# Experts: one more weight chunk in two parts, and the turns of rows at other chunks

## The chip, the cores and the metric

The kernel runs on one core of one Trainium2 chip. Its time is device microseconds of one execution; a figure for a kernel is the median of several executions. All rows below come from one further execution, taken with the hardware profiler.

## The reference

One layer of a streaming encoder: 512 rows of width 1024 in float32. Attention in two head groups comes first, then a mixture of 16 experts. The change is in the experts. What has to be computed there, cut to its core:

```
h2 = _rms(x, norm2_g) * (1.0 + sc2) + sh2
gate = ...                      # top-1 of 4 groups, top-2 of its 4 experts, softmax weights
for e in range(16):
    he = silu(h2 @ w_gate[e]) * (h2 @ w_up[e])      # 1024 -> 512, twice
    y = y + gate[:, e:e+1] * (he @ w_down[e])       # 512 -> 1024
x = x + g2 * y
```

Each expert has 6 MB of weights, some 100 MB in all; they pass through the core once.

## The kernel before

The rows that chose an expert are gathered into one tile of up to 128 rows (`gather_rows`, an indirect DMA of POOL), turned by TensorE so that the features lie on the partitions (`turn`), and written as a high and a low part. The result is scaled by the gate and added to the output by an indirect DMA (`scatter`).

The weights of one expert are 12 **chunks** of 128x1024 values: `g0` to `g3`, `u0` to `u3` (gate and up, two blocks of 128 features each) and `d0` to `d3` (down). The list `CH` sets their order; in the steady part it repeats `u0..u3` of expert e, `g0..g3` of expert e+1, `d0..d3` of expert e. These 12 chunks are called a cycle here. A prime marks the gate chunks of the next expert: g0' to g3'.

A chunk is multiplied in one of two ways:

- **Split.** `chunk_split` (lines 1579 and 1580) makes a high part on ScalarE (`A.copy`, a CAST to fp32r) and a low part on VectorE (`V.tensor_tensor`, a subtraction). `mm3` (lines 235 to 237) then multiplies high by high, low by high and high by low: six matmuls of 512 columns for a chunk.
- **Whole.** The chunk stays in float32 as loaded, and line 1901 multiplies it with the rows in float32: two matmuls, which the trace shows as four records. ScalarE and VectorE do nothing for it. `whole` names the chunks treated so.

Splitting runs four chunks ahead of the matmuls (`AHEAD`). The parts lie in a ring of 11 tiles (`hw`), of which two belong to one chunk; one is given away to a result tile. `late_split` is a table by chunk c: it says whether the split of chunk c+4 is issued before the matmuls of c or after them, and with that where the split stands in the queues of ScalarE and VectorE. Nothing else sorts this part: every engine takes its instructions in the order in which the code issues them.

`raw_load` brings two chunks (1 MB) from memory into one of 12 places; `raw_next` issues the load that reuses a place as soon as both its chunks are used up, so for a split chunk after its split and for a whole chunk after its matmuls.

Five other pieces stand between the chunks:

- `turn(e, q)` for q = 0 and 1: four transposes on TensorE (line 1710), four ACTIVATEs and a CAST on ScalarE (1695, 1697), a subtraction on VectorE (1698, tile `xl`). The half q = 1 feeds chunks 2 and 3 of gate and up.
- `turn_act(e)` after `g1'`: four transposes of the activation (line 1870), a CAST on ScalarE (1873) and a subtraction on VectorE (1874), tile `he`.
- `silu` on ScalarE after `g3` (1924), and the product with the up result on VectorE after `u3` (1927, tile `sl`).
- the `slot_chain` of a later expert: a comparison on VectorE (1658, tile `oh`), four small matmuls (1662, tile `ps_po`), five small instructions on VectorE (1633 to 1640).
- after `d3` two scalings on VectorE (1962, tile `y`) and the scatter.

Of the kernel before, what the change touches and what calls it, by code (L numbers as in the profile page):

```python
# [89 lines left out]
def tile_trunk(ctx, tc, t, out):  # L90
# [45 lines left out]
    def drop(*tiles):  # L136
        for r in tiles:
            ring, k = owner.pop(r.tensor.name)
            spare[ring].append(k)
# [1381 lines left out]

    def whole(nm, j):

        return nm + str(j) in ('g3', 'u3')

    rawt, wsp, held, used = {}, {}, {}, {}
    slots, xs_, eb = {}, {}, {}
# [33 lines left out]
    def raw_next(c):  # L1561

        e, nm, j = CH[c]
        r = RAWS.index((e, nm, j // 2)) + len(PLACES)
        used[r] = used.get(r, 0) + 1
        if used[r] == 2 and r < len(RAWS):
            raw_load(r)

    def chunk_split(c):
        e, nm, j = CH[c]  # L1570
        parts = rawt[e, nm, j // 2][j % 2]
        if whole(nm, j):
            wsp[c] = parts
            return
        hi, lo = wsp[c] = [take("hw", [1024], F32R, n) for n in ("whi", "wlo")]
        n = 1024 // len(parts)
        for k, src in enumerate(parts):
            s = slice(k * n, k * n + n)
            A.copy(hi[:, s], src)  # L1579
            V.tensor_tensor(lo[:, s], src, f32(hi[:, s]), op=OP.subtract)  # L1580
        raw_next(c)
# [16 lines left out]
    def gather_rows(e):  # L1598
        gather(xs_["g"][:, e % 2, :], slots[e][0])
# [12 lines left out]
    def short_values():  # L1612

        v = eb["v16"] = rt.rearrange("p a b c d -> p (a b c d)")[:, 0:NT * NE * 5 // 2].bitcast(BF16).rearrange(
            "p (j e c) -> p j e c", j=NT, e=NE)
        ij = take("t1", [2, NT, NE], name="ij")
        G.iota(ij[:, 0], pattern=[[0, NT], [0, NE]], base=0, channel_multiplier=1, allow_small_or_imprecise_dtypes=True)
        G.iota(ij[:, 1], pattern=[[1, NT], [0, NE]], base=1, channel_multiplier=0, allow_small_or_imprecise_dtypes=True)
        r, f = (take("t1", [NT, NE], name=nm) for nm in ("rest", "part"))
        V.tensor_copy(v[:, :, :, 0:2].rearrange("p j e c -> p c j e"), ij)  # L1620
        src = tv[:, :, :, 2]
        for c in (2, 3, 4):
            V.tensor_copy(v[:, :, :, c], src)
            if c < 4:
                V.tensor_copy(f, v[:, :, :, c])
                V.tensor_tensor(r, src, f, op=OP.subtract)
                src = r
        drop(ij, r, f)
# [20 lines left out]
    def slot_chain(e):  # L1649
        yield need("D", "t2", ("rank", 0))  # L1650
        short = e >= 2
        oh = take("t2", [NT, CAP], BF16 if short else F32, name="oh")

        def sel(lo, hi):

            n = hi - lo
            i3 = iota1.rearrange("p (o w) -> p o w", o=1).broadcast_to([P, n, CAP])
            V.tensor_tensor(oh[:, lo:hi, :], i3, rkp[:, lo:hi, e:e + 1].broadcast_to([P, n, CAP]), op=OP.is_equal)

        def add(j):  # L1660
            v = eb["v16"][:, j, e, :] if short else tv[:, j, e, :]
            PE.matmul(pst[:, 0:v.shape[-1]], oh[:, j, :], v, start=(j == 0), stop=(j == NT - 1))

        if e < 2:
            sel(0, 2)
        if e == 0:
            eb["oh"] = oh
            mark("oh0")
        yield need("D", "", ("rank", 2))
        sel(2 if e < 2 else 0, NT)  # L1670
        if e == 0:
            mark("oh")
        yield need("P", "po", ("gates", 0), ("gates", 2))
        pst = take("po")
        for j in range(NT):
            add(j)
        if e:
            drop(oh)
        yield need("D")
        slots[e] = slot_rows_short(pst, small, e + 1 == NE) if short else slot_rows(pst, small)  # L1680
        drop(pst)
        mark("slots", e)
# [162 lines left out]
    def now(chain):  # L1845
        for _ in chain:
            pass
# [28 lines left out]

    last = []

    late_split = {'u3': 1, 'g2': 1, 'g1': 1, 'd3': 1, 'd1': 1, 'g0': 1}
    pend = []  # L1880
    ahead, ys = {}, []
    yy = page(6, [2, D], name="y")
    for c, (e, nm, j) in enumerate(CH):
        if c + AHEAD < len(CH) and not late_split.get(nm + str(j), 0):
            chunk_split(c + AHEAD)
        late = late_split.get(nm + str(j), 0)
        if c == 0:
            short_values()
        for e1 in range(2, NE):
            d = c - max(12 * e1 - 38, e1 - 2)  # L1890
            if d == 0:
                ahead[e1] = slot_chain(e1)
            for _ in range({0: 3, 3: 1, 4: 1}.get(d, 0)):
                next(ahead[e1], None)
            if e1 == 2 and d == 4:
                gather_rows(2)
        hi, lo = (wsp.pop(c) * 2)[:2]
        if whole(nm, j):
            for kk in range(2):
                src = hi[:, kk * 512:kk * 512 + 512] if hi is lo else (hi, lo)[kk]  # L1900
                PE.matmul(eb[nm, e], eb["xf", e][:, 2 * j + kk - 4, :], src, start=(j == 0 and kk == 0), stop=(j == 3 and kk == 1))  # L1901
            raw_next(c)
            if (nm, j) == ("u", 3):
                drop(eb["xf", e])
        elif nm != "d":
            if j == 0:
                eb[nm, e] = take("mm")
            for kk in range(2):
                kt = 2 * j + kk
                cs = slice(kk * 512, kk * 512 + 512)  # L1910
                mm3(eb[nm, e], xs_["h"][:, e % 2, kt, :], xs_["l"][:, e % 2, kt, :], hi[:, cs], lo[:, cs], kt == 0, kt == 7)
        else:
            if j == 0:
                eb["y", e] = [take("sc"), take("sc")]
            for n in range(2) if e + 1 < NE else (0,):
                cs = slice(n * 512, n * 512 + 512)
                mm3(eb["y", e][n], xs_["he"][:, 0, j, :], xs_["he"][:, 1, j, :], hi[:, cs], lo[:, cs], j == 0, j == 3)
            if e + 1 == NE:
                last.append((hi, lo))
        if not whole(nm, j) and (nm, e) != ("d", NE - 1):  # L1920
            drop(hi, lo)
        if (nm, j) == ("g", 3):
            eb["sl", e] = take("t2", [FE], name="sl")
            A.activation(eb["sl", e], eb["g", e], AF.Silu)
            drop(eb["g", e])
        if (nm, j) == ("u", 3):
            V.tensor_tensor(eb["sl", e], eb["sl", e], eb["u", e], op=OP.mult)
            drop(eb["u", e])
            if e + 1 == NE:
                turn_act(e)  # L1930
        for q in range(2):
            for e1 in (1,) if e < 1 else (e, e + 1, e + 2):
                if e1 >= NE or e1 < 1:
                    continue
                at = ((0, "u", 1 + q)) if e1 == 1 else ((e1 - 1, 'g', 3), (e1 - 1, 'u', 0))[q]
                if at == (e, nm, j):
                    now(turn(e1, q))
                    if q == 1 and e1 + 2 < NE:
                        gather_rows(e1 + 2)
        if (nm, j) == ('g', 1) and e >= 1 and e - 1 + 1 < NE:  # L1940
            turn_act(e - 1)
        if c + AHEAD < len(CH) and late:
            if late == 2:
                pend.append(c + AHEAD)
            else:
                chunk_split(c + AHEAD)
        if late < 2:
            while pend:
                chunk_split(pend.pop(0))
        if (nm, j) == ("d", 0) and e == 3:  # L1950
            count_rounds()
        elif (nm, j) == ("d", 3):
            if e < 3:
                ys.append(take("hw", [D], name="y") if e == 2 else yy[:, e, :])
            y = ys[e % 3]
            for n in range(2):
                cs = slice(n * 512, n * 512 + 512)
                if e + 1 == NE and n:
                    scatter(slots[e][2], y, 0)
                    for k, (hi, lo) in enumerate(last):  # L1960
                        mm3(eb["y", e][n], xs_["he"][:, 0, k, :], xs_["he"][:, 1, k, :], hi[:, cs], lo[:, cs], k == 0, k == 3)
                V.scalar_tensor_tensor(y[:, cs], eb["y", e][n], slots[e][1], rows["g2"][:, cs], op0=OP.mult,  # L1962
                                       op1=OP.mult)
            drop(*eb["y", e])
            if e + 1 == NE:
                scatter(slots[e][3], y, 1)
            else:
                scatter(slots[e][0], y)
# [105 lines left out]
```

## Time and profile before

| what | value |
|---|---|
| time, median of 3 runs | 678.45 us (676.32 to 679.75) |
| time of the profiled execution | 679.67 us |
| its span, first to last instruction | 678.0 us |
| TensorE busy (matmuls) | 639.6 us, 94% |
| VectorE busy | 554.9 us, 82% |
| ScalarE busy | 433.3 us, 64% |
| GpSimd busy | 157.9 us, 23% |
| mean granted TensorE clock | 0.975 of full speed |

The profiled execution lasts 1.67 us longer than its span and stands 1.22 us above the median of the three runs. Shares are means over the whole span; the experts take the last 317 us of it, and there the shares are others. A matmul's record overlaps the next one's, since the engine is pipelined: the distance from start to start is what a matmul costs, not its recorded length. The same holds, by less, for VectorE.

### The profile page before, as it was taken

The page shows a single profiled execution, that of the slowest core. Times are in us where ns is not written, and L with a number is a line of the kernel's source. Part 1 is how long each engine was busy: PE and PEld are TensorE (multiplying, and loading weights), DVE is VectorE, ACT ScalarE, POOL GpSimd, SP SyncE. Part 2 cuts the span into 40 slices and gives each one's busy share as a digit, 9 for nine tenths or more (in the row PEclk, how much of TensorE's full clock was granted, in tenths as well). Part 3 has the DMA queues.
Part 4 walks back from the last instruction along what each step waited for, and adds up shares of the span by engine and source line. Part 5 has one row for each costly group of instructions (what it writes and reads, how often), then busy time and mean ns, then how long its engine had stood idle before and what let it go on. Part 6 is the DMA issues. An engine that isn't in the chain of part 4 may idle for free.

```text
span 678.0 us, 10463 instructions
## 1 busy us (share of the span) xinstructions
PE 639.6 (94%) x3465; PEld 505.5 (75%) x3465; DVE 554.9 (82%) x1229; ACT 433.3 (64%) x835; POOL 157.9 (23%) x230
## 2 busy tenths in 40 slices
PE   8998899999989999999999999999999999999991
PEld 7666798998777876767787677777777777777761
DVE  5768887898887677789988888998988888888870
ACT  6575555755664454433477877777787778777750
POOL 2653021266120001132010111222211022231121
PEclk9798789999998999999999999999999999999996
DMA  8789454036322545237789999999999999999522
GB/s 310 250 249 299 146 194 126 6 102 208 110 71 63 186 175 208 93 125 253 312 309 382 375 346 371 367 370 388 382 395 375 384 368 375 373 370 374 155 31 33
DMA packets 61931, 169.67 MB, mean 250 GB/s; under 512 B 8807, under 2 KB 23629, under 8 KB 54576
## 3 DMA queue, kind: packets, MB, share of 16 engines
q1 hardware_dynamic: 56448, 154.02, 61.2%
q0 software_dynamic: 5376, 14.93, 9.7%
q8 instruction: 28, 0.46, 0.3%
q14 instruction: 31, 0.25, 0.1%
q10 hardware_dynamic: 48, 0.01, 0.0%
HBM read 159.63 MB, written 15.49 MB: 258 GB/s over the span
## 4 chain that ended last, share of the span: by engine, by line
PE 53%; DVE 10%; DMA 3%; ACT 2%; issue 2%; POOL 0%; POOLq 0%; DVEq 0%; ACTq 0%
PE ps_mm L1901 8%; PE ps_mm L235 7%; PE ps_mm L237 7%; PE ps_mm L236 7%; PE ps_sc L235 4%; PE ps_sc L237 4%; PE ps_sc L236 4%; PE ps_tp L1710 2%; DVE acc L1238 2%; DMA xg<-h_d,idx 1%; PE ps_po L887 1%; PE ps_sc L860 1%; PE ps_tp L1870 1%; PE ps_sc L1088 1%; PE ps_tp L874 1%
## 5 line engine op out<-in xcount | busy, mean ns | idle before, releaser
L1580 DVE TENSOR_TENSOR wlo<-wraw,whi 128x1024 fp32r<-128x1024 f32 (+1 forms) x168 | 190.3, 1170 | 8.9 <-ACT whi L1579 8.8
L1579 ACT CAST whi<-wraw 128x1024 fp32r<-128x1024 f32 (+1 forms) x168 | 157.9, 1005 | 0.9 <-PE ps_sc L237 0.5
L1609 POOL DMA_INDIRECT out_dram<-y,idx x15 | 39.9, 2659 | 216.3 <-DVE y L1962 216.3
L235 PE MATMUL ps_mm<-whi,xh 128*128 128x512 f32 x192 | 84.3, 439 | 0.0
L237 PE MATMUL ps_mm<-whi,xl 128*128 128x512 f32 x192 | 75.4, 393 | 0.0
L236 PE MATMUL ps_mm<-wlo,xh 128*128 128x512 f32 x192 | 75.0, 391 | 0.0
L1901 PE MATMUL ps_mm<-wraw,xf 128*128 128x512 f32 x128 | 60.2, 592 | 0.0
L1695 ACT ACTIVATE xf<-ps_tp,norm2x 128x128 f32<-128x128 f32 x120 | 45.1, 462 | 18.2 <-PE ps_tp L1710 18.2
L235 PE MATMUL ps_mm<-whi,hT_hi 128*128 128x256 f32 x192 | 56.7, 295 | 0.0
L236 PE MATMUL ps_mm<-wlo,hT_hi 128*128 128x256 f32 x192 | 55.0, 287 | 0.6 <-DVE wlo L223 0.6
L237 PE MATMUL ps_mm<-whi,hT_lo 128*128 128x256 f32 x192 | 54.8, 285 | 0.0
L235 PE MATMUL ps_sc<-whi,he 128*128 128x512 f32 x128 | 52.8, 412 | 0.7 <-ACT he L1873 0.7
L1238 DVE SCALAR_TENSOR_TENSOR acc<-adaw,s_c,acc 128x512 f32<-128x512 f32 x60 | 47.0, 791 | 4.6 <-DMA adaw<-in_w_ada_dram 3.8
L237 PE MATMUL ps_sc<-whi,he 128*128 128x512 f32 x128 | 50.2, 392 | 0.0
L236 PE MATMUL ps_sc<-wlo,he 128*128 128x512 f32 x128 | 49.9, 390 | 0.0
L236 PEld LDWEIGHTS ps_mm<-wlo,xh 128*128 128x128 f32 x192 | 36.2, 189 | 9.8 <-issue 3.3
L235 PEld LDWEIGHTS ps_mm<-whi,xh 128*128 128x128 f32 x192 | 36.1, 188 | 9.7 <-issue 3.6
L237 PEld LDWEIGHTS ps_mm<-whi,xl 128*128 128x128 f32 x192 | 36.0, 188 | 8.3
L236 PEld LDWEIGHTS ps_mm<-wlo,hT_hi 128*128 128x128 f32 x192 | 37.3, 194 | 1.0 <-DVE wlo L223 0.9
L235 PEld LDWEIGHTS ps_mm<-whi,hT_hi 128*128 128x128 f32 x192 | 37.3, 194 | 0.3
L1873 ACT CAST he<-ps_tp 128x512 fp32r<-128x512 f32 x16 | 9.4, 587 | 43.7 <-PE ps_tp L1870 43.7
L237 PEld LDWEIGHTS ps_mm<-whi,hT_lo 128*128 128x128 f32 x192 | 37.2, 194 | 0.0
(443 smaller groups left out, 1475.0 us busy)
## 6 DMA issues: line engine op xcount, KB each, us to landing
wraw<-in_w_gate_dram SPq DMA_DIRECT2D x32, 1024.0 KB
wraw<-in_w_down_dram SPq DMA_DIRECT2D x32, 1024.0 KB
wraw<-in_w_up_dram SPq DMA_DIRECT2D x24, 1024.0 KB
adaw<-in_w_ada_dram SPq DMA_DIRECT2D x32, 512.0 KB
wraw<-in_w_ada_dram SPq DMA_DIRECT2D x8, 1024.0 KB
wraw<-in_w_up_dram SPq DMA_DIRECT2D x32, 256.0 KB
wraw<-in_w_in_dram SPq DMA_DIRECT2D x12, 512.0 KB
wo<-in_w_o_dram SPq DMA_DIRECT2D x8, 512.0 KB
```

The costliest lines, as they stand in the source:

```text
L235: PE.matmul(o, xh, wh, start=first, stop=False)
L236: PE.matmul(o, xh, wl, start=False, stop=False)
L237: PE.matmul(o, xl, wh, start=False, stop=last)
L860: PE.matmul(s_[:, z * W:(z + 1) * W], qT[h // 4][0:QK + NT, h % 4, qs], kT[h // 4][0:QK + NT, h % 4, 0:W], start=True, stop=True)
L1238: V.scalar_tensor_tensor(acc[0], w[:, z, :], sc, acc[0], op0=OP.mult, op1=OP.add)
L1579: A.copy(hi[:, s], src)
L1580: V.tensor_tensor(lo[:, s], src, f32(hi[:, s]), op=OP.subtract)
L1609: G.indirect_dma_start(out=o, out_offset=bass.IndirectOffsetOnAxis(ap=idx[:, :1], axis=0), in_=y[:, cs], in_offset=None, compute_op=OP.add)
L1695: A.activation(xf[:, kk, :], p3[:, kk, :], AF.Identity, scale=gc, bias=sc)
L1710: PE.transpose(pt[:, kk * P:(kk + 1) * P], xs_["g"][:, e % 2, k0:k0 + P], ident)
L1873: A.copy(xs_["he"][:, 0], p3)
L1901: PE.matmul(eb[nm, e], eb["xf", e][:, 2 * j + kk - 4, :], src, start=(j == 0 and kk == 0), stop=(j == 3 and kk == 1))
```

## The change

Three things change, all in the experts. `g3` leaves the set of whole chunks and is split like the others; `u3` alone stays whole. The table `late_split` has other entries, and the stages of `slot_chain` come one chunk later. The two turns of an expert's rows move: the first from after `g3'` to after `d2` of the same cycle, two experts ahead; the second from after `u0` to after `u2` of the expert before.

```diff
--- before.py
+++ after.py
@@ -1521,7 +1521,7 @@
 
     def whole(nm, j):
 
-        return nm + str(j) in ('g3', 'u3')
+        return nm + str(j) in ('u3',)
 
     rawt, wsp, held, used = {}, {}, {}, {}
     slots, xs_, eb = {}, {}, {}
@@ -1876,7 +1876,7 @@
 
     last = []
 
-    late_split = {'u3': 1, 'g2': 1, 'g1': 1, 'd3': 1, 'd1': 1, 'g0': 1}
+    late_split = {'u3': 1, 'd1': 1, 'g1': 1, 'u0': 1}
     pend = []
     ahead, ys = {}, []
     yy = page(6, [2, D], name="y")
@@ -1887,12 +1887,12 @@
         if c == 0:
             short_values()
         for e1 in range(2, NE):
-            d = c - max(12 * e1 - 38, e1 - 2)
+            d = c - max(12 * e1 - 37, e1 - 2)
             if d == 0:
                 ahead[e1] = slot_chain(e1)
-            for _ in range({0: 3, 3: 1, 4: 1}.get(d, 0)):
+            for _ in range({0: 3, 4: 1, 5: 1}.get(d, 0)):
                 next(ahead[e1], None)
-            if e1 == 2 and d == 4:
+            if e1 == 2 and d == 5:
                 gather_rows(2)
         hi, lo = (wsp.pop(c) * 2)[:2]
         if whole(nm, j):
@@ -1929,10 +1929,10 @@
             if e + 1 == NE:
                 turn_act(e)
         for q in range(2):
-            for e1 in (1,) if e < 1 else (e, e + 1, e + 2):
+            for e1 in (e, e + 1, e + 2):
                 if e1 >= NE or e1 < 1:
                     continue
-                at = ((0, "u", 1 + q)) if e1 == 1 else ((e1 - 1, 'g', 3), (e1 - 1, 'u', 0))[q]
+                at = ((0, "u", 1 + q)) if e1 == 1 else ((e1 - 2, 'd', 2), (e1 - 1, 'u', 2))[q]
                 if at == (e, nm, j):
                     now(turn(e1, q))
                     if q == 1 and e1 + 2 < NE:
```

The first place is TensorE in the ninth cycle, around `g3'`. `whi` and `wlo` are the parts of a split chunk, `wraw` an unsplit one, `xf` the rows in float32, `xh` and `xl` their parts. Before:

```order
L1870 MATMUL ps_tp_7120<-ident,sl_6978 128x128 x4
L235 MATMUL ps_mm_7103<-whi_7088,xh_5429 128x512
L236 MATMUL ps_mm_7103<-wlo_7089,xh_5429 128x512
L237 MATMUL ps_mm_7103<-whi_7088,xl_5430 128x512
L235 MATMUL ps_mm_7103<-whi_7088,xh_5429 128x512
L236 MATMUL ps_mm_7103<-wlo_7089,xh_5429 128x512
L237 MATMUL ps_mm_7103<-whi_7088,xl_5430 128x512
L1901 MATMUL ps_mm_7103<-wraw_6795,xf_7066 128x512 x2
L1710 MATMUL ps_tp_7157<-ident,xg_5312 128x128 x4
L235 MATMUL ps_sc_7173<-whi_7110,he_5431 128x512
L236 MATMUL ps_sc_7173<-wlo_7111,he_5431 128x512
L237 MATMUL ps_sc_7173<-whi_7110,he_5431 128x512
```

The same place in the changed kernel, from the second half of `g2'` on:

```order
L235 MATMUL ps_mm_7185<-whi_7145,xh_5435 128x512
L236 MATMUL ps_mm_7185<-wlo_7146,xh_5435 128x512
L237 MATMUL ps_mm_7185<-whi_7145,xl_5436 128x512
L235 MATMUL ps_mm_7185<-whi_7175,xh_5435 128x512
L236 MATMUL ps_mm_7185<-wlo_7176,xh_5435 128x512
L237 MATMUL ps_mm_7185<-whi_7175,xl_5436 128x512
L235 MATMUL ps_mm_7185<-whi_7175,xh_5435 128x512
L236 MATMUL ps_mm_7185<-wlo_7176,xh_5435 128x512
L237 MATMUL ps_mm_7185<-whi_7175,xl_5436 128x512
L235 MATMUL ps_sc_7241<-whi_7181,he_5437 128x512
L236 MATMUL ps_sc_7241<-wlo_7182,he_5437 128x512
L237 MATMUL ps_sc_7241<-whi_7181,he_5437 128x512
```

Between `g2'` and `d0` there stood the two float32 matmuls of line 1901 and the transposes of a turn; now there stand six matmuls of a split chunk, and the turn has gone.

The second place is VectorE in the same cycle, from the product after `u3` on. Before:

```order
L1927 TENSOR_TENSOR sl_6978<-sl_6978,ps_mm_7054 128x512
L1580 TENSOR_TENSOR wlo_7111<-wraw_6773,whi_7110 128x1024
L1874 TENSOR_TENSOR he_5431<-ps_tp_7120,he_5431 128x512
L1580 TENSOR_TENSOR wlo_7128<-wraw_6773,whi_7127 128x1024
L1658 TENSOR_TENSOR oh_7133<-iota_307,rkp 128x512
L1580 TENSOR_TENSOR wlo_7142<-wraw_6791,whi_7141 128x1024
L1580 TENSOR_TENSOR wlo_7146<-wraw_6791,whi_7145 128x1024
L1698 TENSOR_TENSOR xl_5430<-xf_7162,xh_5429 128x512
L1580 TENSOR_TENSOR wlo_7170<-wraw_6838,whi_7169 128x1024
```

The same stretch now, with one row before it:

```order
L1698 TENSOR_TENSOR xl_5436<-xf_7160,xh_5435 128x512
L1927 TENSOR_TENSOR sl_7050<-sl_7050,ps_mm_7122 128x512
L1580 TENSOR_TENSOR wlo_7176<-wraw_6805,whi_7175 128x1024
L1580 TENSOR_TENSOR wlo_7182<-wraw_6835,whi_7181 128x1024
L1874 TENSOR_TENSOR he_5437<-ps_tp_7198,he_5437 128x512
L1580 TENSOR_TENSOR wlo_7206<-wraw_6835,whi_7205 128x1024
L1580 TENSOR_TENSOR wlo_7212<-wraw_6851,whi_7211 128x1024
L1580 TENSOR_TENSOR wlo_7222<-wraw_6851,whi_7221 128x1024
L1658 TENSOR_TENSOR oh_7227<-iota_307,rkp 128x512
L1580 TENSOR_TENSOR wlo_7238<-wraw_6885,whi_7237 128x1024
L1580 TENSOR_TENSOR wlo_7256<-wraw_6885,whi_7255 128x1024
L1580 TENSOR_TENSOR wlo_7262<-wraw_5493,whi_7261 128x512
```

Behind the product (`sl`) there was one subtraction for the weights ahead of `he`, now there are two; the turn's `xl`, which stood between the subtractions for `d` and those for `u`, stands right before the product, and the comparison `oh` comes behind all four subtractions for `d`.

## Rows read from the trace of the kernel before

**Rows 1.** The page: the span of the profiled execution.

```profile
span 678.0 us, 10463 instructions
```

**Rows 2.** Windows: PE, PEld, DVE, ACT, POOL busy us (instructions), clock, DMA share, GB/s.

```profile
480.00:500.00 20.00, 20.00 (x92) 15.01 (x91) 17.73 (x24) 15.98 (x25) 4.41 (x2) 1.00 1.02 386
620.00:640.00 20.00, 20.00 (x88) 15.11 (x87) 17.09 (x19) 15.02 (x23) 2.29 (x1) 1.00 0.75 242
640.00:660.00 20.00, 18.54 (x77) 13.22 (x76) 15.90 (x17) 11.65 (x14) 4.55 (x1) 1.00 0.23 38
```

**Rows 3.** Waits, 380 to 640 us: us in total, times, longest.

```profile
ACT he L1873 <- PE ps_tp L1870: 35.1, 13, 2.7
...
DVE he L1874 <- ACT he L1873: 13.3, 14, 1.1
DVE wlo L1580 <- ACT whi L1579: 7.7, 30, 0.3
...
DVE xl L1698 <- ACT xh L1697: 5.9, 14, 0.9
```

**Rows 4.** Timeline of PE: start, us, line, operation, count.

```profile
482.39 0.39 PE L235 MATMUL ps_mm<-whi,xh 128*128 128x512 f32 x1
...
483.76 0.60 PE L1710 MATMUL ps_tp<-ident,xg 128*128 128x128 f32 x4
...
486.97 1.88 PE L1901 MATMUL ps_mm<-wraw,xf 128*128 128x512 f32 x4
488.28 0.79 PE L235 MATMUL ps_mm<-whi,xh 128*128 128x512 f32 x1
...
491.82 0.48 PE L235 MATMUL ps_mm<-whi,xh 128*128 128x512 f32 x1
...
493.29 1.88 PE L1901 MATMUL ps_mm<-wraw,xf 128*128 128x512 f32 x4
495.00 0.60 PE L1710 MATMUL ps_tp<-ident,xg 128*128 128x128 f32 x4
...
496.83 0.25 PE L1662 MATMUL ps_po<-rt,oh 128*128 128x5 bf16 x4
496.95 0.48 PE L235 MATMUL ps_sc<-whi,he 128*128 128x512 f32 x1
...
501.12 0.39 PE L235 MATMUL ps_mm<-whi,xh 128*128 128x512 f32 x1
```

**Rows 5.** Timeline of DVE in the same expert.

```profile
483.74 0.16 DVE L1633 COPY sv<-ps_po 128x5 f32<-128x5 f32 x1
...
484.40 1.41 DVE L1962 SCALAR_TENSOR_TENSOR y<-ps_sc,gate,g 128x512 f32<-128x512 f32 x2
485.73 1.22 DVE L1580 TENSOR_TENSOR wlo<-wraw,whi 128x1024 fp32r<-128x1024 f32 x1
486.86 0.68 DVE L1698 TENSOR_TENSOR xl<-xf,xh 128x512 fp32r<-128x512 f32 x1
487.53 2.36 DVE L1580 TENSOR_TENSOR wlo<-wraw,whi 128x1024 fp32r<-128x1024 f32 x2
489.81 0.68 DVE L1927 TENSOR_TENSOR sl<-sl,ps_mm 128x512 f32<-128x512 f32 x1
490.41 1.22 DVE L1580 TENSOR_TENSOR wlo<-wraw,whi 128x1024 fp32r<-128x1024 f32 x1
```

**Rows 6.** Timeline of ACT in the same expert.

```profile
484.39 1.50 ACT L1695 ACTIVATE xf<-ps_tp,norm2x 128x128 f32<-128x128 f32 x4 [1.25 <-PE ps_tp L1710]
485.93 0.62 ACT L1697 CAST xh<-xf 128x512 fp32r<-128x512 f32 x1
```

**Rows 7.** Timeline of PE, first expert: the turn of the second expert's rows.

```profile
371.47 0.63 PE L1710 MATMUL ps_tp<-ident,xg 128*128 128x128 f32 x4 [0.15 <-DMA xg<-h_d,idx]
```

**Rows 8.** Timeline of POOL: the gather that this turn waits for.

```profile
362.12 1.11 POOL L1602 DMA_INDIRECT xg<-h_d,idx  x1 [17.17 <-DVE idx L1595]
```

**Rows 9.** Timeline of ACT near the end: a cast of loaded weights.

```profile
651.48 1.06 ACT L1579 CAST whi<-wraw 128x1024 fp32r<-128x1024 f32 x1 [0.30 <-PE ps_mm L237]
```

## The prediction

> **What bounds the kernel now.** Read first the windows of the expert stage, then the waits of the same stretch, then the timelines of one cycle on each engine.
>
> In a window of 20 us in the middle of the experts TensorE is busy for all 20.00 us at the full granted clock, VectorE for 17.73, ScalarE for 15.98 [rows 2]. Among the waits from 380 to 640 us those of ScalarE and VectorE are for each other or for TensorE, while none of TensorE's own comes near theirs (those that matter here: [rows 3]). So the matmuls set the pace, and VectorE comes next.
>
> The timeline of TensorE gives the cycle: `u0` starts at 482.39 and again at 501.12, so an expert costs 18.73 us [rows 4]. What a piece costs is the distance between starts. The whole chunk `g3'` starts at 493.29 and the turn behind it at 495.00: 1.71 us. Split chunks: `u0` from 482.39 to 483.76 is 1.37; `d1` to `d3` from 496.95 to 501.12 are 4.17, so 1.39 each; `g2'` from 491.82 to 493.29, right behind transposes, is 1.47. The turn before `u1` starts at 483.76.
>
> **The change part by part.**
>
> *TensorE.* In each cycle four float32 records (1.71 us) become six split matmuls. I take 1.39 for them, the mean of three chunks in a row; the ends are 1.37 and 1.47. That saves 0.32 a chunk (0.24 to 0.34). The turns, `he`'s transposes and the small matmuls of line 1662 remain in number and only stand elsewhere. The first turn now stands right before line 1662, where a pause behind it may fall together with the one there: `g2'` behind transposes costs 0.08 more than the mean chunk, so up to 0.1 a cycle is possible; I take none.
>
> How many count: 16 `g3` are split, but the first one's gain is lost. In the first cycle the turn of the second expert's rows starts at 371.47, and the row says that it waited for the gather [rows 7], which POOL issued at 362.12 once VectorE had the row numbers [rows 8]. Those instructions are the same as before, and the chunks ahead of the turn will only wait longer. That leaves 15 x 0.32 = 4.8 us (15 x 0.24 = 3.6 to 15 x 0.44 = 6.6). The new cycle is 18.41 us.
>
> The Trainium skill ("FP8 and Floating Point Precision", TensorE Precision Notes) counts four passes for a float32 matmul; with the 518 cycles at 2.4 GHz that its page "TensorE: Matmul & The Clock Gate" (Back-to-back issue gap) gives for 512 columns, a whole chunk is eight passes, estimated 1.73 us, and a split one six, 1.30, so 15 x 0.43 = 6.5 us saved. The trace agrees on the whole chunk and not on the split one, which takes 1.39.
>
> *ScalarE.* One cast of 1.05 us more in a cycle (the size: [rows 9]). It stands idle for 2.7 us before `he` in most cycles [rows 3], so the cast goes there. Cost nothing; without that room it would be late for VectorE.
>
> *VectorE.* This is the place that can spoil it. Distances between starts [rows 5]: a subtraction for the weights 1.14 (two from 487.53 to 489.81), the two scalings 1.33 (484.40 to 485.73), `xl` 0.67, `sl` 0.60, the five small ones 0.66 (483.74 to 484.40); `he` and `oh` have the same size as `sl`, so 0.60. Before: 10 x 1.14 + 1.33 + 2 x 0.67 + 3 x 0.60 + 0.66 = 16.53 of 18.73. Of the 2.20 left, the three kinds of wait make (13.3 + 7.7 + 5.9) / 14 = 1.92 [rows 3]. Now: 17.67 of 18.41, so 0.74 remain. The waits must shrink, and the order says where: the longest, 1.1 us before `he`, stood behind one subtraction after `sl`; now two stand there, and the new one fills it.
>
> Walk it through with `u0` at 0. TensorE, at 1.39 a chunk and 0.43 for four transposes with the pause behind: turn at 4.17, `u3` 4.60, `g0'` 6.31, `g1'` 7.70, `he`'s transposes 9.09, `g2'` 9.52, `g3'` 10.91, `d0` 12.30, `d1` 13.69, `d2` 15.08, the other turn 16.47. From the start of a turn to the end of ScalarE's work on it are 2.8 us: transposes at 483.76 [rows 4], first ACTIVATE at 484.39, the cast from 485.93 for 0.62 [rows 6]. VectorE therefore: `xl` at 6.97, `sl` 7.64, then the low parts of `g3'` ready at 9.38, `d0` at 10.52, `he` at 11.12, `d1` 12.26, `d2` 13.40, `d3` 14.54, `oh` 15.14, the next `u0` 16.28, `u1` 17.42, `u2` 18.56; then it waits for the second `xl` until 19.27, and with that (19.94), the scalings (21.27), the small ones (21.93) and three subtractions it is at 25.35, when its next `xl` can start at 18.41 + 6.97 = 25.38. It closes, barely. The tightest deliveries are `he`, ready at 11.12 and wanted by the third matmul of `d0` at 12.76, 1.6 us of room, and `g3'`, ready at 9.38 and wanted by its second matmul at 11.14, 1.8 us; `d0` has 2.0. So the low parts arrive in time as long as VectorE's sum stays below the cycle: 18.41 / 17.67 is 4% of margin. Within it the edit costs nothing; beyond it every further per cent costs 0.18 us a cycle.
>
> *Loads.* With `g3` split its load place comes free some four chunks earlier. The queues are full (DMA share 1.02 at 386 GB/s in the middle), but from 640 us on only 38 GB/s are moved [rows 2] while casts of weights go on until 651.48 [rows 9]: the last weights have lain ready for some 11 us, more than the 4.8 that TensorE gains. The gather of later experts is issued two chunks later and wanted three chunks later. Both cost nothing.
>
> *Table and stages.* The other entries of `late_split` move splits by one chunk's work within queues; the walk holds them. Stages of `slot_chain` one chunk later: `oh` is ready at 15.14 and wanted after 16.47.
>
> *Sum.* The profiled execution has a span of 678.0 [rows 1] and a time of 679.67; minus 4.8 it is 674.9. The median of the runs shown lies 1.2 below that execution, so as a median: 678.45 - 4.8 = 673.6 (rounded down; own range 671 to 676, the 3.6 and 6.6 with 1 us of scatter between executions).
>
> **The rivals.**
>
> 1. *VectorE sets the pace: slower.* If a subtraction cannot start 0.08 us before the record of the one before ends, the recorded durations hold: 11 x 1.22 + 1.41 + 5 x 0.68 + 0.80 = 19.03 us a cycle, 0.30 above today's, 15 times: 4.5 us slower, 683. It decides from 18.73 / 17.67, 6% more than my sum. For it: 96% full, and an order in which every wait of 0.7 us counts. Against it: rows 5 show the short distance wherever instructions stand back to back. The Trainium skill ("VectorE: DVE Perf Modes", The DRAIN you can't avoid) says that the next operation does not start until the pipeline is empty, which is this rival; the 1.14 us from start to start beside a record of 1.22 speak against it here.
>
> 2. *No change.* The loads take over: if 386 GB/s is all that there is, a shorter cycle empties the stock and the old 18.73 comes back: 678.4. For it: the DMA share of 1.02. Against it: the stock of 11 us at the end. Or VectorE takes between 4% and 6% more than I count, and the cycle lies between 18.41 and 18.73: 674 to 678.
>
> 3. *It doesn't do what it says.* The order shows six matmuls in place of the four records in every cycle, so this has no weight.
>
> **How the numbers follow.** The forecast gets 72%, rival 1 12%, rival 2 16%. About 0.5%, 3.4 us, is what a measurement of this kernel can tell from no change, so faster means below 675.1. Of the forecast's 72, 64 lie there and 8 above; of rival 2's 16, 3 lie there, 12 within and 1 beyond; rival 1 is slower. That makes 67, 20 and 13. The range for 8 in 10 goes from 670.8 to 678.6: the forecast's own range, a little below, and rival 2; rival 1 is left out.
>
> **What would show it.** `u0` to `u0` at 18.3 to 18.5 us in the changed timeline of TensorE; float32 records halved, from 16 x 2 x 4 = 128 to 64; `g3'` at 1.37 to 1.47; VectorE at over 19 of 20 us in the windows, its wait before `he` gone and one before the first `xl` in its place; the turn of the first cycle still waiting for the gather near 371.5. Wrong would be: matmuls of lines 236 or 237 waiting for `wlo`, a cycle above 18.7, or a wait for a load of weights.

## The result and the profile after

The changed kernel takes 670.2 us (median of 4 runs, 669.26 to 670.74) beside 678.7 for the kernel before on the same chip (4 runs, 676.32 to 679.75): a ratio of 0.988, 95% interval 0.985 to 0.991. That is 8.5 us faster where 4.8 were predicted, and just outside the range. The profiled execution took 670.74, and its span answers to [rows 1]:

```profile
span 669.1 us, 10568 instructions
```

So 8.9 us have gone from the span. The starts in the two timelines of TensorE say where. Before the experts' first matmul 0.6 us went (361.17 against 360.55). Of this 0.45 stands already in matmuls 100 us earlier (248.70 against 248.25), which the change doesn't touch, and in the other profiled kernels this matmul starts anywhere from 358.2 to 361.1: scatter between executions. From that matmul to the second `u0` 2.07 went (27.41 against 25.34); these 16 chunks, `g3` and `g3'` among them, are called the first cycle below. In the fourteen cycles behind it 6.09 went (18.667 against 18.232 on average, 0.435 each), and 0.1 in what follows.

The windows that answer to [rows 2], with the same columns:

```profile
480.00:500.00 20.00, 20.00 (x96) 15.87 (x95) 19.43 (x31) 17.11 (x26) 4.28 (x3) 1.00 1.02 388
620.00:640.00 20.00, 20.00 (x92) 15.90 (x91) 18.37 (x20) 17.66 (x27) 2.29 (x1) 1.00 0.65 226
640.00:660.00 20.00, 13.76 (x56) 9.65 (x54) 10.52 (x13) 4.68 (x6) 7.05 (x3) 0.98 0.28 41
```

TensorE is still busy all the time, now with VectorE at 19.43 of 20 (17.73 before). The waits from 380 to 640 us, as in [rows 3]; each row is us in total, times, longest:

```profile
ACT xf L1695 <- PE ps_tp L1710: 21.8, 28, 1.1
ACT he L1873 <- PE ps_tp L1870: 11.9, 14, 0.9
DVE xl L1698 <- ACT xh L1697: 6.6, 14, 1.0
...
PEld ps_mm L236 <- DVE wlo L1580: 0.5, 2, 0.2
```

ScalarE's wait for `he`'s transposes fell from 35.1 to 11.9, and VectorE's wait before `he` (13.3 before) no longer stands in the view. What VectorE still waits for is one `xl` a cycle. TensorE's weight loads waited for a low part twice in the whole stretch, 0.5 us together.

One cycle of TensorE, as in [rows 4]. The view folds runs of equal instructions; the distance to the next piece is what a piece costs:

```profile
477.62 0.39 PE L235 MATMUL ps_mm<-whi,xh 128*128 128x512 f32 x1
...
481.70 0.60 PE L1710 MATMUL ps_tp<-ident,xg 128*128 128x128 f32 x4
482.14 1.88 PE L1901 MATMUL ps_mm<-wraw,xf 128*128 128x512 f32 x4
483.45 0.79 PE L235 MATMUL ps_mm<-whi,xh 128*128 128x512 f32 x1
484.09 0.40 PE L236 MATMUL ps_mm<-wlo,xh 128*128 128x512 f32 x1
...
486.60 0.60 PE L1870 MATMUL ps_tp<-ident,sl 128*128 128x128 f32 x4
486.95 0.48 PE L235 MATMUL ps_mm<-whi,xh 128*128 128x512 f32 x1
487.27 0.40 PE L236 MATMUL ps_mm<-wlo,xh 128*128 128x512 f32 x1
...
489.78 0.39 PE L235 MATMUL ps_sc<-whi,he 128*128 128x512 f32 x1
...
493.87 0.60 PE L1710 MATMUL ps_tp<-ident,xg 128*128 128x128 f32 x4
494.30 0.24 PE L1662 MATMUL ps_po<-rt,oh 128*128 128x5 bf16 x4
494.41 0.47 PE L235 MATMUL ps_sc<-whi,he 128*128 128x512 f32 x1
494.72 0.39 PE L236 MATMUL ps_sc<-wlo,he 128*128 128x512 f32 x1
...
495.87 0.39 PE L235 MATMUL ps_mm<-whi,xh 128*128 128x512 f32 x1
```

This cycle is 18.25 us (18.25 to 18.33 but for one, until the last three). Three undisturbed chunks, `u0` to `u2` from 477.62 to 481.70, cost 1.36 each. The first turn now shares a place with line 1662 (493.87, 494.30), the second one with `u3`'s float32 matmuls (481.70, 482.14). TensorE now leaves the split matmuls in three places of the cycle, where before it was five (a place is a stretch of other matmuls between split ones). By kind, summed over the distances between starts in one cycle:

| | before | after |
|---|---|---|
| float32 matmuls, line 1901 | 3.03 (8 records) | 1.31 (4) |
| split matmuls | 14.52 (60) | 15.61 (66) |
| transposes | 1.06 (12) | 1.22 (12) |
| line 1662 | 0.11 | 0.11 |
| cycle | 18.73 | 18.25 |

Six split matmuls more cost 1.09, though six undisturbed ones take 1.36: the others have become cheaper by 0.27, of which 0.16 stand with the transposes again (the end of the last transpose counts there when something other than a split matmul follows).

VectorE in the same cycle, as in [rows 5]:

```profile
484.53 0.69 DVE L1698 TENSOR_TENSOR xl<-xf,xh 128x512 fp32r<-128x512 f32 x1
485.14 0.68 DVE L1927 TENSOR_TENSOR sl<-sl,ps_mm 128x512 f32<-128x512 f32 x1
485.74 2.35 DVE L1580 TENSOR_TENSOR wlo<-wraw,whi 128x1024 fp32r<-128x1024 f32 x2
488.01 0.68 DVE L1874 TENSOR_TENSOR he<-ps_tp,he 128x512 fp32r<-128x512 f32 x1
488.81 3.50 DVE L1580 TENSOR_TENSOR wlo<-wraw,whi 128x1024 fp32r<-128x1024 f32 x3
492.22 0.68 DVE L1658 TENSOR_TENSOR oh<-iota,rkp 128x512 bf16<-128x512 f32 x1
```

Counted from `u0` (477.62): `xl` 6.91, `sl` 7.52, `he` 10.39, `oh` 14.60. The walk in the prediction had these four start at 6.97, 7.64, 10.52 and 14.54: all within 0.13. The two subtractions fill the old wait before `he`.

The turn of the second expert's rows in the first cycle, on TensorE, as in [rows 7]:

```profile
369.37 0.60 PE L1710 MATMUL ps_tp<-ident,xg 128*128 128x128 f32 x4
```

POOL's gather for it, as in [rows 8]:

```profile
361.50 1.11 POOL L1602 DMA_INDIRECT xg<-h_d,idx  x1 [17.16 <-DVE idx L1595]
```

The turn waits for nothing. In the kernel before TensorE had waited twice up to here, for `oh` and for the gather, as its waits from 358 to 390 us show:

```profile
PE ps_po L1662 <- DVE oh L1658: 0.7, 1, 0.7
...
PE ps_tp L1710 <- DMA xg<-h_d,idx: 0.2, 1, 0.2
```

Neither wait is left now. The gather was issued 0.62 us earlier, as all of the experts' work, but it landed 2.4 us earlier, at 368.94 against 371.34: it took 7.4 us instead of 9.2.

### The profile page after: what moved, and what is told of

Same layout as the page of the kernel before. It is cut to its first block, busy times and chain, and to the rows that moved or that the text cites. A ratio compares the mean times of both kernels' runs of the same rounds, so it can differ in the third digit from the quotient of the medians.

```text
span 669.1 us, 10568 instructions
## 1 busy us (share of the span) xinstructions
PE 631.6 (94%) x3497; PEld 513.7 (77%) x3497; DVE 569.4 (85%) x1245; ACT 449.5 (67%) x851; POOL 144.3 (22%) x230
## 4 chain that ended last, share of the span: by engine, by line
PE 54%; DVE 10%; ACT 2%; DMA 2%; issue 2%; POOL 0%; POOLq 0%; DVEq 0%; ACTq 0%
PE ps_mm L235 9%; PE ps_mm L237 8%; PE ps_mm L236 8%; PE ps_sc L235 4%; PE ps_sc L237 4%; PE ps_sc L236 4%; PE ps_mm L1901 4%; PE ps_tp L1710 2%; DVE acc L1238 2%; PE ps_po L887 1%; PE ps_mm L1722 1%; PE ps_tp L1870 1%; PE ps_sc L860 1%; PE ps_sc L1088 1%; PE ps_tp L874 1%
## 5 line engine op out<-in xcount | busy, mean ns | idle before, releaser
L1580 DVE TENSOR_TENSOR wlo<-wraw,whi 128x1024 fp32r<-128x1024 f32 (+1 forms) x184 | 205.8, 1172 | 2.6 <-ACT whi L1579 1.0
L1579 ACT CAST whi<-wraw 128x1024 fp32r<-128x1024 f32 (+1 forms) x184 | 174.5, 1012 | 0.6 <-PE ps_sc L237 0.3
L235 PE MATMUL ps_mm<-whi,xh 128*128 128x512 f32 x224 | 95.3, 425 | 0.0
L237 PE MATMUL ps_mm<-whi,xl 128*128 128x512 f32 x224 | 87.6, 391 | 0.0
L236 PE MATMUL ps_mm<-wlo,xh 128*128 128x512 f32 x224 | 87.3, 390 | 0.0
L1609 POOL DMA_INDIRECT out_dram<-y,idx x15 | 28.3, 1886 | 218.4 <-DVE rw L1635 174.0
L236 PEld LDWEIGHTS ps_mm<-wlo,xh 128*128 128x128 f32 x224 | 42.2, 188 | 11.4 <-issue 3.1
L235 PEld LDWEIGHTS ps_mm<-whi,xh 128*128 128x128 f32 x224 | 42.1, 188 | 11.3 <-issue 3.6
L1602 POOL DMA_INDIRECT xg<-h_d,idx x15 | 23.6, 1573 | 32.8 <-DVE idx L1595 17.2
L1901 PE MATMUL ps_mm<-wraw,xf 128*128 128x512 f32 x64 | 30.1, 593 | 0.0
```

Of the source, the lines that this page charges most:

```text
L235: PE.matmul(o, xh, wh, start=first, stop=False)
L236: PE.matmul(o, xh, wl, start=False, stop=False)
L237: PE.matmul(o, xl, wh, start=False, stop=last)
L1602: G.indirect_dma_start(out=d, out_offset=None, in_=h2_d, in_offset=bass.IndirectOffsetOnAxis(ap=idx[:, :1], axis=0), bounds_check=S - 1, o ...
L1609: G.indirect_dma_start(out=o, out_offset=bass.IndirectOffsetOnAxis(ap=idx[:, :1], axis=0), in_=y[:, cs], in_offset=None, compute_op=OP.add)
```

## The experiments

Two things were open: why a cycle gained 0.435 us instead of 0.32, and why the first cycle gained at all. Of the cycle, theory P: the chunk is worth 0.35, and the rest comes from fewer places at which TensorE leaves the split matmuls, each with a pause of about 0.09 us and some settling. Theory V: VectorE stands so near its limit that its margin, not TensorE's matmuls, decides what a part of the change is worth. Of the first cycle, theory L: splitting `g3` lets a load of weights (of the second expert's `d2` and `d3`) be issued before the gather instead of behind it, and the gather is faster by that. "Cycle" below is the mean from the second `u0` to the sixteenth, in one profiled execution of each kernel; ratios are against runs of the kernel before on the same chip.

**Splitting `g3` alone.** The kernel before, with one line changed:

```diff
-        return nm + str(j) in ('g3', 'u3')
+        return nm + str(j) in ('u3',)
```

> The kernel before with g3 split and nothing else changed (turns, slot stages and table as before). Theory P (pauses): a split chunk costs its six matmuls at 0.227 us, 1.36, wherever it stands, and each place where the stream of split matmuls is broken costs a pause of its own. Here one chunk changes from 1.71 to 1.36 and no break goes away: 0.35 a cycle, cycle 18.36 to 18.40, some 5 to 6 us below the kernel before (672.5 to 673.5). Rival V (VectorE): the old turns and table leave no room for the added subtraction, TensorE waits for low parts, cycle above 18.55, 675.5 or more. Rival S (the split alone): cycle 18.25 to 18.30 and 670 to 671, as in the changed kernel.

674.12 us, ratio 0.995 (0.993 to 0.997). The cycle is 18.334: 0.333 less. The first cycle is 27.17, 0.24 less, though its gather took 7.3 us. The waits of TensorE from 358 to 390 us say why:

```profile
PE ps_po L1662 <- DVE oh L1658: 0.7, 1, 0.7
PE ps_tp L1710 <- DMA xg<-h_d,idx: 0.6, 1, 0.6
```

Ahead of the turn TensorE still waited for `oh` (0.72 us, at 365.09), and behind it, at 381.00, for the next gather, that of the third expert's rows, which are wanted behind `g3'`. So the chunk gives a little over half of the whole, and the earlier gather shows hardly anything in the first cycle while these waits stand. Most cycles (18.37 to 18.42) are near what P expected; the total is 0.6 us above its range.

**The rows alone.** The changed kernel, with `g3` whole and the old table, so that only the turns and the stages differ from before:

```diff
-        return nm + str(j) in ('u3',)
+        return nm + str(j) in ('g3', 'u3')
-    late_split = {'u3': 1, 'd1': 1, 'g1': 1, 'u0': 1}
+    late_split = {'u3': 1, 'g2': 1, 'g1': 1, 'd3': 1, 'd1': 1, 'g0': 1}
```

> The changed kernel with g3 whole again and the table as before: only the turns and the slot stages stand where the change puts them. Theory P: two breaks fall together with others (turn with u3, turn with the slot matmuls), so the cycle falls from 18.73 by 0.06 to 0.13, to 18.60 to 18.67, and the first cycle loses its wait for oh of some 0.7; 675.5 to 677.5. Rivals V and S: the moves only make room on VectorE, or do nothing: cycle 18.70 to 18.75, 677.5 to 679.

677.73, ratio 0.998 (0.996 to 1.000). The cycle is 18.629, 0.04 less. The first cycle is 26.66, 0.75 less, as P expected: the wait for `oh` is gone, and the turn then waits 0.36 us for the gather, which took 8.7 us. Two places go (a turn to line 1662, a turn to `u3`), and one is new, since the first turn no longer stands behind `g3'`. One place net, 0.04 us: P has the right sign, and less than its 0.09. From the last `u0` on, the profiled execution took 1.5 us more than that of the kernel before; the granted clock there was 0.69 from 656 to 660 us.

**Stages one chunk earlier.** The changed kernel, with the stages of `slot_chain` where they were:

```diff
-            d = c - max(12 * e1 - 37, e1 - 2)
+            d = c - max(12 * e1 - 38, e1 - 2)
-            for _ in range({0: 3, 4: 1, 5: 1}.get(d, 0)):
+            for _ in range({0: 3, 3: 1, 4: 1}.get(d, 0)):
-            if e1 == 2 and d == 5:
+            if e1 == 2 and d == 4:
```

> The changed kernel with the slot stages one chunk earlier again, two chunks ahead of the first turn: the small matmuls of line 1662 stand alone between d0 and d1 and no longer right behind the turn's transposes. Theory P: one more break, 0.09 for its pause and some 0.03 for the matmuls behind it: cycle 18.36 to 18.42 against 18.28, 1.3 to 2 us above the changed kernel (671.5 to 672.2). Rivals V and S: nothing depends on where these four stand, 670.2 within 0.5.

680.64, ratio 1.004 (1.002 to 1.006); the cycle is 18.98 to 19.05 until the last three (18.783 on average). This missed what P expected, and the waits from 380 to 640 us say why:

```profile
DVE xl L1698 <- ACT xh L1697: 15.1, 27, 1.0
PEld L1662 <- DVE oh L1658: 11.1, 12, 1.4
...
PE ps_po L1662 <- DVE oh L1658: 6.4, 12, 1.0
```

The matmuls of line 1662 come before VectorE has done `oh`, and TensorE stands for half a microsecond in each cycle. With `g3` split and the turns moved, the later stages are no detail.

**The old table.** The changed kernel with the old `late_split`:

```diff
-    late_split = {'u3': 1, 'd1': 1, 'g1': 1, 'u0': 1}
+    late_split = {'u3': 1, 'g2': 1, 'g1': 1, 'd3': 1, 'd1': 1, 'g0': 1}
```

> The changed kernel with the old late_split table. Theory P and S: the table only shifts splits within VectorE's and ScalarE's room, cycle 18.25 to 18.32, 670.2 within 0.6. Rival V: the table is what keeps VectorE in time; TensorE waits for low parts, and the time is 2 us or more above the changed kernel.

671.05, ratio 0.990 (0.988 to 0.991); the cycle is 18.233, the first one 25.75 instead of 25.34. In the two profiled executions the table is worth 0.4 us, all in the first cycle; the medians lie 0.85 apart.

**All chunks split.** `u3` too, so that no float32 matmul is left:

```diff
-        return nm + str(j) in ('u3',)
+        return False
...
```

> The changed kernel with u3 split as well, so that no chunk is whole. If TensorE's stream alone counted (theory P without VectorE), u3 would save another 0.36 a cycle: cycle 17.92, 665 to 666. Theory V-limit: VectorE's sum by start distances becomes 17.67 + 1.14 = 18.81 us a cycle, more than TensorE needs, so the cycle is 18.7 to 18.9 with TensorE waiting for low parts or for sl, 675.5 to 678.5.

681.02, ratio 1.004 (1.002 to 1.005). The cycles lie between 18.69 and 19.34 until the last two (18.793 on average), as V-limit expected; the total is 2.5 us above its range, and from the last `u0` on the profiled execution took 3 us more than the changed kernel's, with the granted clock at 0.50 to 0.68 from 656 to 664 us. In the waits TensorE now stands for VectorE (the edit moves lines up by one), and in the window VectorE, not TensorE, comes nearest to 20:

```profile
PEld ps_tp L1870 <- DVE sl L1926: 13.9, 14, 1.1
PE ps_tp L1870 <- DVE sl L1926: 8.0, 13, 0.7
```

```profile
480.00:500.00 20.00, 19.34 (x94) 15.58 (x93) 19.67 (x27) 17.83 (x28) 3.27 (x2) 1.00 1.02 373
```

One subtraction more (1.14 us), and VectorE's sum of 17.67 becomes 18.81, more than TensorE's cycle: V holds here. VectorE does set the pace, as the prediction's first rival has it, one chunk further on; but it does so by the sum of its start distances, without that rival's condition that the longer recorded durations hold.

**The load late.** The changed kernel, with that one load issued behind `g3`'s matmuls as before:

```diff
-        raw_next(c)
+        if c != 3:
+            raw_next(c)
...
+        if c == 3:
+            raw_next(c)
```

> The changed kernel with one load of 1 MB (the second pair of down chunks of the second expert) issued after the matmuls of the first expert's g3 instead of behind its split, as in the kernel before. Theory L (load order): this load, issued some 8 us earlier and ahead of the other loads, is why the first gather takes 7.4 us in the changed kernel and 9.2 before; back in its old place the gather takes 8.7 to 9.3 us, the turn of the second expert's rows waits for it, and the first cycle is 1 to 1.8 us longer (26.4 to 27.1 against 25.34); 671.2 to 672. Rival: the gather's time is chance or goes by something else: 7.2 to 7.5 us and 670.2 within 0.5.

672.51 (670.01 to 677.26), ratio 0.992 (0.989 to 0.995). By the totals the step is not resolved; by the first cycle it is: 26.98 instead of 25.34, with the other cycles as they were (18.233, where the changed kernel has 18.232). The turn waits again (its line is one further down here):

```profile
368.64 0.63 PE L1711 MATMUL ps_tp<-ident,xg 128*128 128x128 f32 x4 [1.48 <-DMA xg<-h_d,idx]
```

The gather, issued at 359.14, took 9.4 us. In the ten kernels profiled with the early load it took 7.2 to 7.7 us, in the three with the late one (before, the rows alone, this) 8.7 to 9.4. L holds.

From the experts' first matmul to this turn it takes 10.30 us in the kernel before, 9.76 with `g3` split alone, 9.76 with the rows alone, 8.82 in the changed kernel and 10.44 with the load late. So the earlier gather gives its gain only where the wait for `oh` is gone too. With the load late the first cycle is 0.43 us shorter than in the kernel before, all of it behind the turn.

**Joining the third place.** The changed kernel, with the first turn's transposes and line 1662's matmuls right behind those for `he`, and ScalarE's and VectorE's part of the turn left behind `d2`:

```diff
-            d = c - max(12 * e1 - 37, e1 - 2)
+            d = c - {2: 0, 3: 1, 4: 11, 5: 16}.get(e1, 12 * e1 - 49)
-            for _ in range({0: 3, 4: 1, 5: 1}.get(d, 0)):
+            for _ in range({0: 3, (a := 4 if e1 < 5 else 6 if e1 == 5 else 11): 1, a + 1: 1}.get(d, 0)):
...
             turn_act(e - 1)
+            if e + 1 < NE:
+                hold[e + 1] = turn(e + 1, 0)
+                for _ in range(2):
+                    next(hold[e + 1])
...
-                    now(turn(e1, q))
+                    now(hold.pop(e1) if (q == 0 and e1 > 1) else turn(e1, q))
```

> The changed kernel with the breaks of TensorE's stream joined further: from the fifth expert on the transposes of the first turn and the four slot matmuls stand right behind those of turn_act, so two places a cycle are broken instead of three; ScalarE's and VectorE's part of the turn stays after d2. Theory P: 0.09 to 0.14 a cycle less, 18.13 to 18.20, 668.2 to 669.2. Rival: the break costs nothing of its own, 670.2 within 0.5; or VectorE, 96% full, is upset by the small instructions' new place and TensorE waits, 671 or more.

676.22, ratio 0.997 (0.995 to 0.998). The cycle is 18.169, 0.06 less than in the changed kernel and less than P's number; the first one is 32.73, since the third expert's rows are now wanted long before they can be there (the edit moves the first turn's transposes from these rows on; line 1662's matmuls join them only from the sixth expert on):

```profile
382.37 1.09 PE L1710 MATMUL ps_tp<-ident,xg 128*128 128x128 f32 x4 [4.78 <-DMA xg<-h_d,idx]
```

Behind this wait the granted clock was 0.50, the lower of its two levels, from 382 to 386 us, and until 387.10 the split matmuls started 0.43 us apart instead of 0.23. Wait and clock together make up most of the 7.4 us.

**The first turn one chunk earlier.** Behind `d1` instead of `d2`, and so a place of its own again:

```diff
-                at = ((0, "u", 1 + q)) if e1 == 1 else ((e1 - 2, 'd', 2), (e1 - 1, 'u', 2))[q]
+                at = ((0, "u", 1 + q)) if e1 == 1 else ((e1 - 2, 'd', 1), (e1 - 1, 'u', 2))[q]
```

> The changed kernel with the first turn after d1 instead of d2, one chunk ahead of the slot matmuls, which stay before d3: one more break of the stream, with oh as late as it was. Theory P: 0.09 to 0.14 a cycle more, 18.37 to 18.42, 671.4 to 672.2. Rival: where the breaks stand costs nothing, 670.2 within 0.5. Should TensorE wait for oh or for low parts, that shows as a wait and counts for neither.

678.12, ratio 0.999 (0.998 to 1.001). The cycle is 18.756, 0.52 more than in the changed kernel, far above P's number for one place. From 390 to 640 us:

```profile
DVE xl L1698 <- ACT xh L1697: 11.7, 12, 1.8
...
PEld ps_tp L1870 <- DVE sl L1927: 5.9, 12, 0.7
```

ScalarE's part of the turn now stands ahead of the casts for `u1` and `u2`; VectorE waits for `xl` up to 1.8 us at a stretch, and TensorE's weight loads then wait for `sl` and, by 5.4 us in the same view, for low parts. A place cannot be measured by moving work that VectorE has a part in. The next kernels leave VectorE out.

**Joined in the middle only.** The kernel of the third place, with the join for experts 6 to 14 alone:

```diff
             turn_act(e - 1)
+            if 6 <= e + 1 < NE - 1:
+                hold[e + 1] = turn(e + 1, 0)
...
```

> The changed kernel with the first turn of rows and the slot matmuls moved right behind the transposes before he for experts 6 to 14 alone; the early experts and the last stay as in the changed kernel. Theory P (each place where TensorE leaves the split matmuls costs about 0.09 us and some settling): the cycles of these nine experts take 18.17 to 18.20 us where the changed kernel has 18.23, the first cycle and the tail stay at 25.3 and 13.7 us, so about 0.4 us less than the changed kernel: 669.8. If the 7 us that the first cycle lost when all experts were joined came from the early gathers alone, nothing of that loss is left. Rival: joining disturbs VectorE wherever it stands, then the cycle where it begins takes over 19 us and the sum is 671 or more.

670.03 (5 runs), ratio 0.989 (0.987 to 0.991). The joined cycles take 18.21 to 18.24 until the last ones, a little above P's 18.17 to 18.20, where the changed kernel's go between 18.25 and 18.33, and the first cycle (25.35) and the end are as there. So the loss of the full join was that of the first experts. It beats the kernel before; from the changed kernel the totals don't tell it apart.

**Transposes in a place of their own, and beside others.** The changed kernel with four more 128x128 transposes per cycle whose result nobody reads, in the one behind `d0`, in the other behind `d2` with the turn:

```diff
+        if (nm, j) == ("d", 0) and 1 <= e:
+            pt = take("tp")
+            for kk in range(4):
+                PE.transpose(pt[:, kk * P:(kk + 1) * P], ident, ident)
+            drop(pt)
```

> The changed kernel with four extra 128x128 transposes behind d0 of experts 1 to 15, whose result nobody reads: one more place per cycle where TensorE leaves the split matmuls, and no work for any other engine. Theory P: own time 0.35 us and a pause with settling of 0.08 to 0.14, so 0.43 to 0.49 a cycle: cycle 18.66 to 18.72, total 676.7 to 677.6. Rival (no pause, the transposes cost their own time wherever they stand): 0.35 a cycle, the same as in the next kernel, 675.5.

> The same four extra transposes per cycle, right ahead of the turn behind d2, so that no further place is added. Theory P: only their own time, 0.33 to 0.36 a cycle: cycle 18.56 to 18.60, total 675.2 to 675.7, which is 0.08 to 0.14 a cycle less than with the transposes apart. Rival: no difference between the two places.

Apart: 676.77, cycle 18.686. Beside: 676.86, cycle 18.641; from the last `u0` on this profiled execution took 1.6 us more than the one apart, where the granted clock fell to 0.76. The totals don't tell the two places apart. The cycles do, by 0.04 in nearly every one and 0.045 on average, which is half of what P expected. First the timeline of the one apart, then of the one beside (line 1943 holds the added transposes):

```profile
491.76 0.60 PE L1943 MATMUL ps_tp<-ident 128*128 128x128 f32 x4
492.12 0.48 PE L235 MATMUL ps_sc<-whi,he 128*128 128x512 f32 x1
492.43 0.40 PE L236 MATMUL ps_sc<-wlo,he 128*128 128x512 f32 x1
492.67 0.40 PE L237 MATMUL ps_sc<-whi,he 128*128 128x512 f32 x1
492.90 0.40 PE L235 MATMUL ps_sc<-whi,he 128*128 128x512 f32 x1
```

```profile
494.54 0.60 PE L1710 MATMUL ps_tp<-ident,xg 128*128 128x128 f32 x4
494.97 0.60 PE L1943 MATMUL ps_tp<-ident 128*128 128x128 f32 x4
495.41 0.24 PE L1662 MATMUL ps_po<-rt,oh 128*128 128x5 bf16 x4
```

Beside others, four transposes cost 0.43 to 0.44. Apart they seem to cost 0.36, and the split matmul behind them 0.31 instead of 0.23: 0.44 again. The "pause" is the end of the last transpose, which the view books on its successor, and it is paid in either place. What a place does cost is the settling: the twelve split matmuls from 492.12 to the next turn at 494.98 take 2.86 us; twelve at 0.227 and the 0.09 of the transpose are 2.81. That leaves 0.05.

So of P the pause falls and the settling stands, 0.04 to 0.06 us a place on average (0.04 from the rows alone, 0.06 from the join, 0.045 from these two). It can also be summed directly: what the split matmuls take beyond 0.227 from start to start, without the first one behind another kind, is 0.17 us a cycle in the kernel before, 0.20 with `g3` split alone, 0.10 in the changed kernel and 0.04 with the third place joined (eleven cycles from the second `u0` on). The 0.435 of a cycle are then 0.333 for the chunk, as split alone, and 0.10 for two places joined.

## Why the prediction was wrong

- *What bounds the kernel.* Right: TensorE before and after, VectorE next.
- *The chunk* (1.71 to 1.39, 0.32). Nearly right, in part by luck; alone it gave 0.333. The six added matmuls cost 1.36, which would be 0.35, and 0.02 went to more settling; my mean of `d1` to `d3` had the end of line 1662's break in it. For the Trainium skill's 518 cycles for 512 columns ("TensorE: Matmul & The Clock Gate", Back-to-back issue gap), estimated 0.216 us a matmul, the trace has 0.227 even undisturbed.
- *The turns* ("up to 0.1 a cycle is possible; I take none"). This term of the sum was mis-sized: it is 0.10, 1.4 us over the cycles. The view showed what a chunk costs behind other matmuls, and I could have counted places: five and three. My reason, two pauses that fall together, was not the right one; the pause doesn't go, the settling does.
- *The first cycle* ("the first one's gain is lost"). This step failed. I held that the instructions before the gather are the same and took its arrival with them. But the part on the loads says that `g3`'s load place comes free earlier, and I did not ask what the load that goes there does to the gather: 7.4 us instead of 9.2. With that load back in its old place the first cycle gains 0.43, near the 0.32 that the sum has there (for `g3'`). And the wait for `oh`, 0.74 us ahead of that turn in the kernel before, went with the later stages, to which I gave nothing. Together the first cycle gave 2.07: up to the turn 1.48, where split and moves alone give 0.54 each, and behind it 0.60. Of this the moves alone give 0.21, and `g3'` some 0.32 once the wait of 0.62 is taken off that the split has when it stands alone. The sign that I named, a turn still waiting near 371.5, did not come.
- *VectorE.* Right, to 0.13 us for the four starts shown, and at 19.43 of 20 as forecast. Splitting `u3` as well shows the limit at the place where the sum has it. The section of the Trainium skill that my first rival names ("VectorE: DVE Perf Modes", The DRAIN you can't avoid) goes on to say that an operation that is not held starts earlier, so it does not stand for the rival alone; the trace fits this part, with 1.14 us from start to start beside records of 1.22.
- *ScalarE, loads of weights, table.* Right: none cost anything that shows in TensorE's waits; the table gave some 0.4 us.
- *The stages* ("`oh` is ready at 15.14 and wanted after 16.47"). True, but the remark hid what they are for: without them the whole gain is lost, some 10 us.
- *The range.* Its lower end had 0.44 a cycle and 1 us of scatter. The fourteen cycles came to that end (6.09; 14 x 0.44 = 6.16), the first cycle gave 2.07 where the sum had 0.32 to 0.44, and 0.6 lies before the experts. So the span lost 4.1 us more than the sum: 1.75 in the first cycle, 1.6 in the fourteen others, 0.7 outside both.

## What to carry to other kernels

Count the places at which the engine that sets the pace changes its kind of work, before and after, and price each; small work moved beside other small work gained 0.04 to 0.06 us a place here. When a buffer comes free earlier, ask which load is then issued earlier and which small transfer with a waiting reader it now stands ahead of or behind. When an engine is at 97%, a part of a change that costs nothing may be what holds the rest: try the change without it.

## What the runs showed of the hardware

- Undisturbed split matmuls of 512 columns start every 0.227 us. Behind transposes, line 1662 or float32 matmuls five to ten of the next mostly start 0.224 to 0.236 apart, some 0.02 to 0.05 us together. It is not so every time: behind line 1662 in the kernel before (496.95) they start 0.227 apart from the second on. Why was not tried.
- Four 128x128 float32 transposes cost 0.44 us, wherever they stand. Behind the four float32 records of `u3` the first split matmul takes 0.64 us (483.45 to 484.09), 0.41 more than an undisturbed one. This, too, is no pause: with the 1.31 before it this makes 1.72, and the same four records cost 1.71 where a transpose follows them ([rows 4], 493.29 to 495.00).
- After TensorE had stood for 4.78 us the granted clock was 0.50, and split matmuls started 0.43 us apart (the third place joined, from 383.68 on).
- The same gather of rows took 7.2 to 7.7 us with a weights load issued before it and 8.7 to 9.4 with that load issued while it ran. Whether it is the queue or the memory that makes it slow is open.
